# First layer's modulation by VectorE row sums instead of narrow matmuls, and its gate and branch weights' low parts by adding transfers

## The chip, the core and the metric

The kernel runs on one core of a Trainium2 chip. The metric is the device time of one execution in microseconds, as the median of several runs. A core has TensorE (PE, with a queue PEld that loads weights), VectorE (DVE), ScalarE (ACT), GpSimd (POOL) and SyncE (SP), which work in parallel, each in the order of its own queue, and sixteen DMA engines that move data between the main memory (HBM) and the on-chip SBUF. In this kernel plain transfers are issued by SP, and adding transfers, which add their source onto what lies at their destination, by POOL.

## The reference, cut to what matters

Two layers over 256 latent tokens `x` and 256 context tokens `xc`, 1024 channels wide. Per layer, all in float32:

```python
mod = s_lat @ w_ada[l] + b_ada[l]      # silu(c) @ (1024 x 6144); mod_c likewise from c_ctx
sh1, sc1, g1, sh2, sc2, g2 = split(mod, 6)
h = rmsnorm(x) * (1 + sc1) + sh1       # hc likewise from xc
p = h @ w_in[l]                        # 1024 -> 4608: conv branch | q, k, v | two gates
y_conv = conv_branch(p[..., :1024])    # GLU, 31-tap depthwise conv, LayerNorm, swish, @ w_conv_out
y_attn = attention(q, k, v, ...) @ w_na_out[l]
x = x + g1 * ((sigmoid(gc) * y_conv + sigmoid(ga) * y_attn) @ w_out[l])
h2 = rmsnorm(x) * (1 + sc2) + sh2
x = x + g2 * conv_ffn(h2)              # 1024 -> 5632, width-3 conv, gate, 2816 -> 1024
```

In the first layer the context tokens go the same way; in the last they serve only as keys and values. The output is the latent stream after a last RMSNorm.

The change concerns the modulation vectors `mod` of the first layer, from `g1` up to `sc2`, for both streams (two vectors of 1024 by a 1024 x 1024 block for each of the three parts), and the way in which the first layer's gate, attention-projection and convolution-projection weights are made ready for TensorE.

## The kernel before, in words

**Weights and products.** Activations lie with the channels on the 128 partitions. All weights but the modulation's come as units of 128 x 1024 float32 (512 KB): `U_IN + t` is tile `t` of the input projection (`T_GATE + n`, `t` = 14 to 29, are the sixteen gate tiles), `U_NA`, `U_CO` and `U_WO` are the attention, convolution and output projections. Each unit is loaded into a `raw` place (four of them) and split into a high part `whi` and a low part `wlo` (four places each), and each product is three matmuls (`mm3`, L187 to L189): high by high, high by low, low by high. For 512 tokens a gate unit is one `group` of 24 matmuls of 512 columns; a branch unit (`branch`) holds two groups of 12.

**Two ways to a low part.** `wunit` casts on ACT (L168) and subtracts on DVE (L169). `wadded` casts on ACT (L206), writes the negated high part into `wlo` on ACT (L207), and has POOL issue a transfer that adds `raw` onto it (L208). `unit8` chooses by the set `ADDED`. Before, it holds the first 19 tiles of the first layer's input projection (up to the fifth gate) and some of the second layer's. Branch units always take `wunit`.

**Two ways to the modulation.** `ada_all` computes a chunk of 256 outputs for both streams on TensorE: two units loaded into `raw`, sixteen matmuls of 32 output rows each (`ada_half`, L220), a copy on ACT (`ada_rows`, L239), two transposes and a small sum on DVE (`ada_sums`, L246 to L256). `ada_dots` computes a tile of 128 outputs on DVE: one unit is loaded (L155, in `raw_unit`), and for each stream one `tensor_tensor_reduce` (L289) multiplies it by the broadcast vector (`sb0`, made by `across`) and sums along the row straight into `mods`. In the first layer, chunks 0 to 7 (shift and scale of the first norm) are done at the start by TensorE and are not touched; chunks 8 to 12 (tiles 16 to 25) by `ada_all`, and tiles 26 to 39 by `ada_dots`.

**Order.** The program is written out in one stream, and its scheduler gives each engine its queue. Background work consists of generators in `side`; each `slot()` advances all of them by one step, and a group of 512 columns has two slots. `pace[0]` sets how many row sums `ada_dots` may do per slot: for two streams, a pace of 1.2 makes 0.6 tiles a slot. In the first layer the stretch around the change is: the last eleven gates (with the convolution's taps and LayerNorm as background work), the attention projection `U_NA` into the gates (L980), the convolution projection `U_CO` and the merge into `z` (L985 to L988), then the output projection `U_WO`, four units for both streams and four units for one stream after the other, with the residual (L993) that reads `g1`. `finish(g1)` runs what is left of the row sums before the second norm, which needs `sc2` and `sh2`.

Of the kernel before, what the change touches and what calls it, by code (L numbers as in the profile page):

```python
# [8 lines left out]
F32 = mybir.dt.float32  # L9
# [6 lines left out]
P = 128  # L16
# [3 lines left out]
S = 256  # L20
# [11 lines left out]
UW = 1024  # L32
# [11 lines left out]

U_GLU0, U_V, U_IN, U_NA, U_CO, U_WO, U_UP, U_DN = 0, 2, 6, 36, 40, 44, 52, 96
NU = 118
ADDED = {*((0, U_IN + i) for i in range(19)), *((1, U_IN + i) for i in (7, 8, 9, 14, 15, 16, 17))}
T_GLU, T_Q, T_K, T_GATE = 0, 6, 10, 14

SWAP16 = [(i + 16) % 32 for i in range(32)]  # L50
# [3 lines left out]
def trunk(ctx: ExitStack, tc: tile.TileContext, xt, cvec, crow, wall, wada, params, bias_t, rope_t, out):  # L54
# [34 lines left out]
    def add_side(gen):  # L89
        side.append(gen)  # L90
# [168 lines left out]
    def ada_all(chunks, rest=0):  # L259
        for l, j in chunks:  # L260
            ev = ada_rows(ada_products(l, j, "sc"))
            yield
            yield
            ada_sums(l, j, ev)
            for _ in range(rest):
                yield
# [9 lines left out]
    pace = [1.0]  # L276
# [336 lines left out]
    for l in range(DEPTH):  # L613
# [5 lines left out]
        with ExitStack() if last else start as e1a:  # L619
# [81 lines left out]
            with ExitStack() as e1b:  # L701
# [191 lines left out]
                n = 0  # L893
# [16 lines left out]
            with ExitStack() as e1c:  # L910
                ec = e1c.enter_context(tc.tile_pool(name=f"ec{l}", bufs=1))

                if l == 0:
                    sb0 = [across(ec, s) for s in range(2)]

                    def ada_more():
                        yield from ada_all([(0, 8)])
                        yield from ada_dots(0, range(26, 40), sb0)

                    pace[0] = 0.6  # L920
                    g1 = ada_more()
                    add_side(g1)
                sh_ = [ec.tile([P, T], F32R, name=f"sh{l}_{j}") for j in range(KC)]
                sl_ = [ec.tile([P, T], F32R, name=f"sl{l}_{j}") for j in range(KC)]

                def layer_norm():

                    while taps:
                        for _ in range(6 if last else 5):
                            if taps:  # L930
                                conv_tap(*taps.pop(0))
                        yield
                    pace[0] = 1.0 if last else 0.6
                    flat = [c.rearrange("p s t -> p (s t)") for c in cb]
                    sm = tp.tile([P, 512], F32, tag="ss", name=nm("ss"))
                    eng = pool if last else dve
                    eng.tensor_tensor(sm[:, :T], flat[0], flat[1], ALU.add)
                    eng.tensor_tensor(sm[:, :T], sm[:, :T], flat[2], ALU.add)
                    dve.tensor_tensor(sm[:, :T], sm[:, :T], flat[3], ALU.add)
                    yield  # L940
                    pm = psum("po")
                    pe.matmul(pm[:, :T], one.to_broadcast([P, P]), sm[:, :T], start=True, stop=True)
                    (s2,) = sum_squares(1, T)
                    for j in range(KC):
                        dve.scalar_tensor_tensor(flat[j], pm[:, :T], -1.0 / CONV, flat[j], ALU.mult, ALU.add)
                        s2.add(flat[j], j == KC - 1)
                    for _ in range(2 if last else 4):
                        yield
                    pb = yield from rstd(s2, CONV, "po")
                    for j in range(KC):  # L950
                        sg = tmp()
                        g, b = pr(l, LNG + j, 1), pr(l, LNB + j, 1)
                        dve.scalar_tensor_tensor(flat[j], flat[j], g, pb[:, :T], ALU.mult, ALU.mult)
                        act.activation(sg[:, :T], flat[j], AF.Sigmoid, bias=b)
                        dve.scalar_tensor_tensor(flat[j], flat[j], b, sg[:, :T], ALU.add, ALU.mult)
                        act.copy(sh_[j], flat[j])
                        dve.tensor_tensor(sl_[j], flat[j], sh_[j].bitcast(F32), ALU.subtract)
                        yield
                    pace[0] = 0.4 if last else 0.6

                side.remove(conv)
                ln = layer_norm()
                add_side(ln)
                for n in range(n, 2 * KD):
                    gate(ec, n, False)


                z = h_tiles()
                if not last:
                    g2 = ada_all([(0, j) for j in range(9, 13)], 4)  # L970
                    add_side(g2)

                def branch(base, xh, xl):
                    for n in range(0, KD, 2):
                        w = wunit(l, base + n // 2)
                        for i in range(2):
                            yield n + i, group(psum(), [cols(w, 4 * i + k) for k in range(KC)], xh, xl, ALL)

                for n, pa in branch(U_NA, oh, ol):
                    dve.tensor_tensor(gates[KD + n], pa[:, :T], gates[KD + n], ALU.mult)  # L980
                finish(ln)
                pace[0] = 0.0
                for n, pc in branch(U_CO, sh_, sl_):
                    t = tmp()[:, :T]
                    dve.tensor_tensor(t, pc[:, :T], gates[n], ALU.mult)  # L985
                    dve.tensor_tensor(t, t, gates[KD + n], ALU.add)
                    act.copy(z[0][n][:, :T], t)
                    dve.tensor_tensor(z[1][n][:, :T], t, z[0][n][:, :T].bitcast(F32), ALU.subtract)  # L988


                def residual(ss_, ps, part, n, s, off):
                    c = slice(s * S, (s + 1) * S)
                    dve.scalar_tensor_tensor(x[n][:, c], ps[:, off : off + S], mod(l, part, n, s), x[n][:, c], ALU.mult, ALU.add)  # L993
                    ss_.add(x[n][:, c], n == KD - 1)

                h2 = z

                RAW = slice(S, 2 * S + 2)

                def plain(k):  # L1000
                    hi, lo = z[0][k][:, CTX], z[1][k][:, CTX]
                    g = gains[l, 4][:, k, 0:1]
                    lastev[0] = act.activation(hi, x[k][:, LAT], AF.Identity, scale=g)
                    dve.scalar_tensor_tensor(lo, x[k][:, LAT], g, hi.bitcast(F32), ALU.mult, ALU.subtract)

                def plain_shift(k):
                    hi, lo = (z[i][k][:, 2 * S : 2 * S + 2] for i in range(2))
                    b = mod(l, 3, k, 0).to_broadcast([P, 2])
                    act.copy(hi, b)
                    dve.tensor_tensor(lo, b, hi.bitcast(F32), ALU.subtract)  # L1010

                if not last:
                    finish(g2)
                sss = sum_squares(NS, S)
                if last:
                    for k in range(KD):
                        gain(l, 4, N2G, k, 1)
                        plain_shift(k)
                NB = KD if last else KD // 2
                for n in range(NB):  # L1020
                    ps = group(psum(), unit8(l, U_WO + n), *z, ALL)
                    for s in range(NS):
                        residual(sss[s], ps, 2, n, s, s * S)
                    if last:
                        plain(n)
                    elif n == 0:
                        pace[0] = 0.8
                pace[0] = 0.3
                held = [unit8(l, U_WO + n) for n in range(NB, KD)]
                for s in range(NS if held else 0):  # L1030
                    for n, w in zip(range(NB, KD), held):
                        c = slice(s * S, (s + 1) * S)
                        ps = psum()
                        for k in range(KD):
                            mm3(ps[:, c], w[k], z[0][k][:, c], z[1][k][:, c], k == 0, k == KD - 1)
                            if k % 4 == 3:
                                slot()
                        residual(sss[s], ps, 2, n, s, s * S)
                    if s == 0:
                        finish(g1)  # L1040
                        nl = norm(l, sss[0], 4, 3, N2G, h2, (0,))
                        add_side(nl)
# [187 lines left out]
def _ada_units(w):  # L1230

    import numpy as np

    u = np.ascontiguousarray(w.transpose(0, 2, 1)).reshape(DEPTH, 48, P, UW).copy()
    u[0, :16] = w[0][:, : 2 * D].reshape(2, 4, P, 2, 8, P).transpose(4, 0, 2, 1, 3, 5).reshape(16, P, UW)
    u[0, 16:26] = w[0].reshape(2, 4, P, 24, S).transpose(3, 0, 2, 1, 4)[8:13].reshape(10, P, UW)
    return u


# [90 lines left out]
```

## Time and profile before

| | |
|---|---|
| median of 3 runs | 1120.04 us (1119.17 to 1121.54) |
| profiled execution, its own time | 1121.22 us |
| its span in the profile | 1119.4 us |
| granted TensorE clock, mean | 0.997 |
| HBM read | 187.63 MB, 169 GB/s over the span |
| loads by SP (plain) | 190.77 MB in the queue q1 |
| adding transfers by POOL | 26 of 512 KB, 13.63 MB in the queue q0 |

In a row by line, "x1328 | 446.7, 337" is count, busy time in us and mean ns of one; behind the next bar stands the idle time of the engine just before, and what ended it. In a row of order in time the first two numbers are start and duration. A row of a stage has its bounds, its length, and then the busy time of each engine with the number of instructions. A row of waits has the total, the number of times, and the longest. Durations of matmuls overlap: the time that one costs PE is the distance between starts. The DMA share is the mean busy share of the sixteen engines.

### The profile page before, as it was taken

What the parts mean: (1) busy time and instruction counts of PE and PEld (TensorE: products, weight loads), DVE (VectorE), ACT (ScalarE), POOL (GpSimd) and SP (SyncE); (2) the same over time, 40 slices, a digit from 0 to 9 for tenths busy, and PEclk for the clock granted to TensorE, in tenths of its full rate; (3) what the DMA queues carried; (4) which work ended last, traced back from release to release, by engine and by line L of the source; (5) the groups of instructions that cost most, each with busy time, mean ns of one, the idle gap of its engine ahead of it and who ended that gap; (6) DMA issues with size and microseconds to landing.
All of it is one profiled execution on the core that took longest, in us unless ns stands there. A gap on an engine that the chain in (4) does not pass through costs nothing.

```text
span 1119.4 us, 18214 instructions
## 1 busy us (share of the span) xinstructions
PE 1103.7 (99%) x6988; PEld 954.0 (85%) x6988; DVE 886.9 (79%) x1615; ACT 582.8 (52%) x968; POOL 36.2 (3%) x50
## 2 busy tenths in 40 slices
PE   9999999999999999999999999999999999999997
PEld 7777777787789988888888788998899999999997
DVE  5579899875878788887997655789699898988773
ACT  3458878541334543434334222545778667666642
POOL 1011110000000000000000000000100000000000
PEclk9999999999999999999999999999999999999998
DMA  9988662554743354544556666566864474666781
GB/s 345 298 191 228 146 166 82 188 166 158 256 136 116 114 166 143 176 157 144 169 173 205 207 192 206 183 201 193 230 180 148 154 254 161 192 196 179 219 271 57
DMA packets 59223, 205.60 MB, mean 184 GB/s; under 512 B 7168, under 2 KB 7424, under 8 KB 59136
## 3 DMA queue, kind: packets, MB, share of 16 engines
q1 hardware_dynamic: 55104, 190.77, 53.6%
q0 software_dynamic: 3744, 13.63, 6.3%
q8 instruction: 55, 0.90, 0.3%
q14 instruction: 32, 0.26, 0.1%
q10 hardware_dynamic: 288, 0.04, 0.0%
HBM read 187.63 MB, written 1.05 MB: 169 GB/s over the span
## 4 chain that ended last, share of the span: by engine, by line
PE 83%; DVE 7%; ACT 5%; DMA 3%; issue 1%; SPq 1%; DVEq 0%; ACTq 0%
PE main L187 24%; PE main L189 24%; PE main L188 24%; PE main L724 4%; DMA raw<-in_wall 2%; DVE cb L654 2%; SPq L716 1%; DVE wlo L169 1%; PE sc L187 1%; PE sc L189 1%; PE sc L188 1%; PE po L555 1%; ACT whi L168 1%; PE po L220 1%; DMA x<-in_xt 1%
## 5 line engine op out<-in xcount | busy, mean ns | idle before, releaser
L187 PE MATMUL main<-h,whi 128*128 128x256 f32 (+1 forms) x1328 | 446.7, 337 | 0.0
L189 PE MATMUL main<-h,wlo 128*128 128x256 f32 (+1 forms) x1328 | 442.9, 335 | 1.1 <-DVE wlo L169 1.1
L188 PE MATMUL main<-h,whi 128*128 128x256 f32 (+1 forms) x1328 | 442.4, 334 | 0.1
L168 ACT CAST whi<-raw 128x1024 fp32r<-128x1024 f32 (+1 forms) x218 | 225.4, 1038 | 261.2 <-DMA raw<-in_wall 139.6
L169 DVE TENSOR_TENSOR wlo<-raw,whi 128x1024 fp32r<-128x1024 f32 (+1 forms) x218 | 262.4, 1209 | 100.6 <-ACT whi L168 99.1
L187 PEld LDWEIGHTS main<-h,whi 128*128 128x128 f32 x1328 | 249.4, 188 | 30.7 <-issue 2.6
L189 PEld LDWEIGHTS main<-h,wlo 128*128 128x128 f32 x1328 | 249.3, 188 | 29.6 <-DVE wlo L169 1.5
L188 PEld LDWEIGHTS main<-h,whi 128*128 128x128 f32 x1328 | 249.8, 188 | 28.7 <-DVE h L385 0.5
L654 DVE SCALAR_TENSOR_TENSOR cb<-u,par,cb 128x512 f32<-128x512 f32 (+1 forms) x240 | 144.9, 618 | 3.0
L289 DVE CUSTOM_DVE_ANT_0 t<-raw,sb,par 128x1024 bf16<-128x1024 f32 x100 | 126.7, 1279 | 2.2 <-DMA raw<-in_wada 2.2
L189 PE MATMUL main<-fh,wlo 128*128 128x256 f32 (+1 forms) x386 | 123.0, 319 | 0.4 <-DVE wlo L169 0.4
L188 PE MATMUL main<-fl,whi 128*128 128x256 f32 (+1 forms) x386 | 123.0, 319 | 0.0
L187 PE MATMUL main<-fh,whi 128*128 128x256 f32 (+1 forms) x386 | 122.9, 319 | 0.0
L189 PEld LDWEIGHTS main<-fh,wlo 128*128 128x128 f32 x386 | 72.7, 188 | 6.4 <-DVE wlo L169 0.9
L187 PEld LDWEIGHTS main<-fh,whi 128*128 128x128 f32 x386 | 72.7, 188 | 5.6
L188 PEld LDWEIGHTS main<-fl,whi 128*128 128x128 f32 x386 | 72.7, 188 | 5.6
L1058 ACT ACTIVATE t<-main,par 128x512 f32<-128x512 f32 (+1 forms) x82 | 50.7, 668 | 28.0 <-PE main L189 28.0
L1059 DVE SCALAR_TENSOR_TENSOR t<-main,par,t 128x510 f32<-128x510 f32 (+1 forms) x82 | 47.5, 615 | 7.0 <-ACT t L1058 6.7
L1062 DVE SCALAR_TENSOR_TENSOR t<-main,par,t 128x510 f32<-128x510 f32 (+1 forms) x82 | 46.6, 610 | 0.0
L384 ACT ACTIVATE h<-t,mod 128x256 fp32r<-128x256 f32 x56 | 25.4, 502 | 37.6 <-DVE t L383 37.6
L724 PE MATMUL main<-whi,h 128*128 128x512 f32 x128 | 40.5, 402 | 0.1
L1084 ACT CAST fh<-t 128x256 fp32r<-128x256 f32 (+1 forms) x43 | 21.9, 510 | 34.6 <-DVE t L1074 34.2
(224 smaller groups left out, 1253.2 us busy)
## 6 DMA issues: line engine op xcount, KB each, us to landing
raw<-in_wall SPq DMA_DIRECT2D x239, 512.0 KB, 4.3
raw<-in_wada SPq DMA_DIRECT2D x88, 512.0 KB, 4.6
wlo<-raw POOLq DMA_DIRECT2D x26, 512.0 KB, 5.8
bias<-in_bias_t SPq DMA_DIRECT2D x8, 520.0 KB, 5.5
row<-in_wada SPq DMA_DIRECT2D x8, 512.0 KB, 5.3
sb<-in_crow SPq DMA_DIRECT2D x5, 512.0 KB, 5.7
x<-in_xt SPq DMA_DIRECT2D x8, 256.0 KB, 4.5
raw<-in_wall SPq DMA_DIRECT2D x8, 256.0 KB, 7.9
```

The lines of the kernel that those rows point to most:

```text
L168: act.copy(hi[:, c], r[:, c])
L169: dve.tensor_tensor(lo[:, c], r[:, c], hi[:, c].bitcast(F32), ALU.subtract)
L187: pe.matmul(ps, w[0], xh, start=start, stop=False)
L188: pe.matmul(ps, w[0], xl, start=False, stop=False)
L189: pe.matmul(ps, w[1], xh, start=False, stop=stop)
L289: dve.tensor_tensor_reduce(tmp().bitcast(BF16), r, v, 1.0, pr(l, BADA + n, 1), ALU.mult, ALU.add, mods[l][:, n, s : s + 1])
L384: high = act.activation(hi[:, c], y[:, c], AF.Identity, bias=b)
L654: dve.scalar_tensor_tensor(cb[j], src, w, cb[j], ALU.mult, ALU.add)
L724: mm = pe.matmul(pv[t], h1[n == 1][k][:, c], w[n == 2][:, b], start=k + n == 0, stop=k == KD - 1 and n == 2)
L1058: act.activation(c, pv_, AF.Identity, bias=pr(l, FDB + t, 1), scale=w[1])
L1059: dve.scalar_tensor_tensor(c[:, :, 1:], pv_[:, :, : S - 1], w[0], c[:, :, 1:], ALU.mult, ALU.add)
L1062: dve.scalar_tensor_tensor(c[:, :, : S - 1], pv_[:, :, 1:], w[2], c[:, :, : S - 1], ALU.mult, ALU.add)
```

## The change

Row sums on VectorE take over tiles 16 to 25 of the first layer's modulation: `ada_dots` runs from tile 16 to 39, with the paces changed to 1.2 in the gates, 0.7 in `U_NA` and 0.2 in `U_CO`. Its loads get two places of their own (`own`) instead of the four `raw` ones. The five chunks of `ada_all` with their matmuls, copies and transposes are gone there. The first layer's remaining eleven gate units and its eight `U_NA` and `U_CO` units get their low parts by adding transfers. The layout of the modulation's weights follows (tiles 16 to 25 lie as those after them).

```diff
-ADDED = {*((0, U_IN + i) for i in range(19)), *((1, U_IN + i) for i in (7, 8, 9, 14, 15, 16, 17))}
+ADDED = {*((0, U_IN + i) for i in range(30)), *((1, U_IN + i) for i in (7, 8, 9, 14, 15, 16, 17))}
...
                     sb0 = [across(ec, s) for s in range(2)]
 
-                    def ada_more():
-                        yield from ada_all([(0, 8)])
-                        yield from ada_dots(0, range(26, 40), sb0)
-
-                    pace[0] = 0.6
-                    g1 = ada_more()
+                    own = lambda: ec.tile([P, UW], F32, tag="own", bufs=2, name=nm("own"))
+                    pace[0] = 1.2
+                    g1 = ada_dots(0, range(16, 40), sb0, own)
                     add_side(g1)
...
-                    pace[0] = 1.0 if last else 0.6
+                    pace[0] = 1.0 if last else 1.2
...
-                    pace[0] = 0.4 if last else 0.6
+                    if last:
+                        pace[0] = 0.4
...
                 z = h_tiles()
-                if not last:
-                    g2 = ada_all([(0, j) for j in range(9, 13)], 4)
-                    add_side(g2)
 
                 def branch(base, xh, xl):
                     for n in range(0, KD, 2):
-                        w = wunit(l, base + n // 2)
+                        w = wunit(l, base + n // 2) if last else wadded(l, base + n // 2)
...
+                if not last:
+                    pace[0] = 0.7
                 for n, pa in branch(U_NA, oh, ol):
...
                 finish(ln)
-                pace[0] = 0.0
+                pace[0] = 0.0 if last else 0.2
                 for n, pc in branch(U_CO, sh_, sl_):
...
-                if not last:
-                    finish(g2)
                 sss = sum_squares(NS, S)
...
-    u[0, 16:26] = w[0].reshape(2, 4, P, 24, S).transpose(3, 0, 2, 1, 4)[8:13].reshape(10, P, UW)
```

## The prediction

> **What bounds the kernel now.** I read the page first (sums by engine, chain), then the engines by stage around the change, then the waits of that stretch, then TensorE in order of time, then DMA by stage. In the page:
>
> ```profile
> PE 1103.7 (99%) x6988; PEld 954.0 (85%) x6988; DVE 886.9 (79%) x1615; ACT 582.8 (52%) x968; POOL 36.2 (3%) x50
> ...
> PE 83%; DVE 7%; ACT 5%; DMA 3%; issue 1%; SPq 1%; DVEq 0%; ACTq 0%
> ```
>
> TensorE is busy for 99% of the span, and 83% of the chain that ended last is its work. The change touches the stretch from layer 0's sixth gate to the middle of its output projection, here cut at the gates, the attention projection (U_NA), the convolution projection (U_CO) and the start of the output projection (columns: PE, PEld, DVE, ACT, POOL, granted clock, DMA share, GB/s):
>
> ```profile
> 197.00:262.00 65.00, 65.00 (x297) 51.73 (x297) 46.22 (x68) 28.68 (x40) 1.96 (x1) 1.00 0.49 162
> 262.00:290.00 28.00, 27.24 (x155) 19.94 (x154) 19.05 (x36) 4.77 (x7) 0.00 (x0) 1.00 0.69 231
> 290.00:314.00 24.00, 24.00 (x118) 19.03 (x117) 20.83 (x32) 11.22 (x15) 0.00 (x0) 1.00 0.64 212
> 314.00:348.00 34.00, 34.00 (x201) 29.79 (x200) 25.78 (x50) 9.36 (x18) 0.00 (x0) 1.00 0.43 124
> ```
>
> PE is full, at a granted clock of 1.00; DVE, ACT and DMA have room. The waits between 196 and 348 us hold a single line in which PE's matmuls stood for somebody:
>
> ```profile
> ACT whi L168 <- PE main L188: 26.8, 12, 5.0
> ...
> PE main L189 <- DVE wlo L169: 0.8, 1, 0.8
> ```
>
> The first line says that the preparation of weights runs ahead: twelve times ACT stood at a whi place that PE had not yet given back, so units are made ready as early as four places allow. So here time is what PE executes, and a microsecond taken off PE is a microsecond of the kernel, as long as nothing new is late for PE.
>
> **What the change takes off PE.** Five chunks of the modulation (8 to 12 of layer 0) go: each is 16 narrow matmuls (L220) and, later, two transposes (L246) among the wide ones. One of them, in order of time on PE:
>
> ```profile
> 263.06 0.40 PE L189 MATMUL main<-oh,wlo 128*128 128x512 f32 x1
> 263.39 1.07 PE L220 MATMUL sc<-raw,sil 128*32 128x256 f32 x16
> 264.39 0.50 PE L187 MATMUL main<-oh,whi 128*128 128x512 f32 x1
> 264.73 0.39 PE L188 MATMUL main<-ol,whi 128*128 128x512 f32 x1
> ...
> 267.04 0.39 PE L189 MATMUL main<-oh,wlo 128*128 128x512 f32 x1
> 267.27 0.38 PE L246 MATMUL pt<-ident,t 128*128 128x128 f32 x2
> 267.40 0.48 PE L187 MATMUL main<-oh,whi 128*128 128x512 f32 x1
> 267.72 0.40 PE L188 MATMUL main<-ol,whi 128*128 128x512 f32 x1
> ```
>
> Durations overlap, so I go by starts. From 264.73 to 267.04 lie ten wide matmuls: 0.231 us each. From 263.06 to 264.73 are two such steps (0.46) in 1.67 us: the 16 narrow matmuls cost 1.21. From 267.04 to 267.72 are two steps in 0.68 us: the transposes cost 0.22. Together 1.43 us a chunk, 5 x 1.43 = 7.1 us.
>
> The one wait is also in this stretch:
>
> ```profile
> 276.50 0.39 PE L188 MATMUL main<-ol,whi 128*128 128x512 f32 x1
> 277.65 0.50 PE L189 MATMUL main<-oh,wlo 128*128 128x512 f32 x1 [0.76 <-DVE wlo L169]
> ```
>
> 1.15 us between two starts instead of 0.23: 0.9 us. A low part of a branch unit came late, from VectorE. After the change no low part before U_WO is VectorE's, and the modulation's loads no longer take two of the four raw places at a time until PE has read them. It goes, unless an added transfer is late in its stead. The most that can be won is 7.1 + 0.9 = 8.0 us.
>
> **What the change adds, and what hides it.** Prices, from the groups by form:
>
> ```profile
> L169 DVE TENSOR_TENSOR wlo<-raw,whi 128x1024 fp32r<-128x1024 f32 x212 | 258.4, 1224 | 100.3 <-ACT whi L168 99.1 <-PE po L942 0.2
> L289 DVE CUSTOM_DVE_ANT_0 t<-raw,sb,par 128x1024 bf16<-128x1024 f32 x100 | 126.7, 1279 | 2.2 <-DMA raw<-in_wada 2.2
> L207 ACT ACTIVATE wlo<-whi 128x1024 fp32r<-128x1024 f32 x26 | 27.7, 1065 | 0.4
> L289 DVE DVE_READ_ACCUMULATOR2_ANT mod<- 128x1 f32 x108 | 8.9, 83 | 0.0
> L208 POOL DMA_DIRECT2D wlo<-raw x26 | 22.8, 877 | 197.8 <-ACT wlo L207 94.1 <-PE pt L246 34.0 <-ACT qk L864 31.9
> ```
>
> VectorE: row sums for tiles 16 to 39 instead of 26 to 39, ten tiles for two streams: 20 x (1.279 + 0.083) = 27.2 us more. Eleven gate units and eight branch units lose their subtraction: 19 x 1.224 = 23.3 us less. Net +3.9 us, with five reductions, five bias adds and no more evictions on ACT to set against it. By stage:
>
> ```profile
> 197.00:262.00 65.00, 12.77 (x11) 1.00 0.49 162
> ...
> 197.00:262.00 65.00, 15.05 (x24) 1.00 0.49 162
> 262.00:290.00 28.00, 10.13 (x16) 1.00 0.69 231
> ```
>
> The first line is L169, the others L289; 24 rows are twelve sums with their read-outs, six tiles, so a tile is 2.51 us. A pace of 1.2 gives 0.6 tiles a slot; the eleven gates have 22 slots, 12 tiles or 30.1 us. VectorE then has 46.2 - 12.8 - 15.1 + 30.1 = 48.4 us in a stage of 11 x 24 x 0.231 = 61 us. In U_NA (16 slots at 0.7, 5.6 tiles) it has 14.1 us of sums and what it had beside its 10.1 us of sums and its subtractions, some 5 us, in 22 us. Both fit, though U_NA only just. What VectorE gives PE there is a free bank (L980), and three further banks cover 3 x 12 x 0.231 = 8.3 us of lateness. I take zero.
>
> ACT: 19 x 1.065 = 20.2 us more, over some 105 us in which it is at most half busy. POOL: 19 issues of 0.88 us on an idle engine. I take zero for both.
>
> SP: ten tiles' loads (512 KB each) replace the same ten units of the chunks, but wait for one of two places of their own. The wait that this takes away and the one that stays, among SP's waits between 200 and 300 us:
>
> ```profile
> SPq L155 <- PE sc L220: 13.4, 4, 8.3
> ...
> SPq L155 <- DVE mod L289: 4.4, 3, 2.2
> ```
>
> Behind a modulation load in SP's queue stand the weight loads. Before, they stood up to 8.3 us behind a load that waited for the narrow matmuls. Afterwards they stand behind one that waits for the row sum two tiles earlier; the waits for a sum here are 2.2 us at the longest. Between 0 and the ten loads times 2.2 us, less the 13.4 that go; a raw place is filled some four units (22 us) ahead, so I take zero.
>
> DMA is the term that is not zero. A few microseconds in layer 1 where plain loads and adding transfers run together (775 to 800 us), and the gates stage as it is:
>
> ```profile
> q1 hardware_dynamic: 995, 3.65, 46.8%
> q0 software_dynamic: 576, 2.10, 43.5%
> raw<-in_wall SPq DMA_DIRECT2D x7, 512.0 KB, 5.8
> wlo<-raw POOLq DMA_DIRECT2D x5, 512.0 KB, 7.3
> ...
> q1 hardware_dynamic: 2880, 10.49, 48.9%
> raw<-in_wada SPq DMA_DIRECT2D x9, 512.0 KB, 4.5
> raw<-in_wall SPq DMA_DIRECT2D x9, 512.0 KB, 4.0
> ```
>
> An adding transfer costs 0.435 x 25 us / 2.10 MB x 0.524 MB = 2.7 us of all sixteen engines; a load costs 0.489 x 65 / 10.49 x 0.524 = 1.6 us. Gates and U_NA together: 15 units x (1.6 + 2.7) + 17.6 tiles x 1.6 = 93 us in 84 us of PE. That is 9 us too much, a tenth. Against it stand the cushions. A whi place comes free four units ahead, 3 x 5.5 = 16.6 us before PE needs it; cast, negated copy, issue and a landing of 7.3 us take 1.05 + 1.07 + 0.88 + 7.3 = 10.3 us; 6.3 us are left. The raw place ahead of it has about as much again, and modulation tiles may lag without PE noticing. In the 25 us quoted, 5.8 and 7.3 us to landing with the engines 90% taken made no wait of PE. I take 1.5 us of PE waiting for an added low part, nearer to nothing than to the 9 us; the ends are 0 and 9.
>
> The Trainium skill, "DMA: Bandwidth & Descriptors", section "Anatomy of one DMA", gives a fixed 2 us and bytes over 436 GB/s. At that rate 512 KB occupy the engines for 1.2 us, an estimate, loads and adds alike, and the same sum is 15 x 2.4 + 17.6 x 1.2 = 57 us of 84: no excess, and the full 8.0 us. The trace does not agree for adding transfers, 2.7 us each.
>
> **The sum.** 8.0 - 1.5 = 6.5 us. The profiled execution took 1121.22 us for a span of 1119.4; it becomes 1114.7. It lies 1.2 us above the median of the runs, 1120.04, and so the median becomes 1113.5 us. PE stays full after 348 us, so nothing later takes it back. About 0.2%, 2.2 us, is what a measurement here can tell from no change.
>
> **Rivals.** *Everything is hidden*: the DMA excess is taken up by the cushions, 8.0 us, 1112.0. For it: PE waits for no added low part in the trace of before. It is the good end of my case. *VectorE becomes the bound in U_NA*: it works in order, and a sum whose tile has not landed holds the L980 behind it. If VectorE enters U_NA more than the 8.3 us of three banks late, PE waits. Its 48.4 us of 61 speak against this. It would return 3 to 5 us: 1117. *The sixteen DMA engines become the bound*, which ends on the other side: in gates and U_NA every unit takes what its transfers take. It decides once the backlog is over the 6.3 us of the whi places and the lag of the tiles doesn't help, since their loads stand ahead of the weights' in SP's queue. Priced by the rows: 9 us of excess and, because a late unit also holds its raw place and the next load behind it, about 3 us more in refilling: 12 - 8.0 = 4 us slower, 1124. For it: 69% of the engines' time was already taken in U_NA before any adding transfer. Against: those in layer 1 at 90% without a wait. The same page, section "Issuing engines are not separate DMA queues", says that transfers issued by different engines interleave on the same sixteen, which would make POOL's transfers lengthen SP's; the trace agrees as far as it goes, with loads landing in 5.8 us beside adds and 4.0 without.
>
> **How the numbers follow.** My case with its good end, 1111.5 to 1116: 0.60. VectorE, 1116 to 1119: 0.15. DMA as the bound, 1119 to 1128: 0.25, of which 0.05 under 1122.3. Faster by over 0.2% (under 1117.8): 0.60 and most of the second, 0.70. Slower (over 1122.3): 0.20. Between: 0.10. The range of 8 in 10 leaves a little below 1111 and the upper end of the DMA case: 1111 to 1123. The forecast's own range is 1111.5 to 1116.
>
> **What would show it.** In the profile after: no L220 on bank sc after 60 us and 16 transposes of L246 instead of 26; 45 added transfers instead of 26; L169 with 19 fewer; 128 row sums in all, over both forms. Right: PE has under 2 us of idle time between 197 and 340 us, all for wlo by DMA. Wrong by DMA: the share in gates and U_NA is near 1.0, landings of wlo over 10 us, and PE waits for them. Wrong by VectorE: PE waits for L980. Wrong in the first term: U_NA starts less than 1.2 us earlier after the gates, which hold one chunk.

## The result, and the profile after

The changed kernel takes 1132.05 us (median of 6 runs, 1130.02 to 1134.8) against 1121.32 us before (6 runs, 1119.17 to 1123.27). The ratio is 1.0097, interval 1.008 to 1.0114: slower by 10.7 us, where 1113.5 us was forecast. The profiled execution has a span of 1130.4 us, 11.0 more than before.

The sums and the chain, from the page of the changed kernel:

```profile
PE 1100.1 (97%) x6898; PEld 954.0 (84%) x6898; DVE 889.0 (79%) x1626; ACT 599.1 (53%) x982; POOL 52.8 (5%) x69
...
PE 76%; issue 7%; DVE 5%; DMA 5%; ACT 5%; SPq 1%; POOL 0%; POOLq 0%; DVEq 0%; ACTq 0%
```

TensorE is busy for 3.6 us less, and for 97% of the span instead of 99%: it stands. By stage (length, PE, PEld, DVE, ACT, POOL, granted clock, DMA share, GB/s):

```profile
197.00:219.00 22.00, 22.00 (x95) 17.43 (x94) 15.01 (x25) 16.93 (x23) 3.89 (x5) 1.00 0.98 252
219.00:234.00 15.00, 8.26 (x40) 6.69 (x39) 7.82 (x14) 4.98 (x6) 3.56 (x3) 0.83 0.87 264
234.00:268.00 34.00, 34.00 (x145) 27.40 (x144) 19.85 (x32) 17.48 (x24) 4.57 (x6) 0.98 0.94 235
268.00:278.00 10.00, 10.00 (x46) 8.18 (x44) 5.00 (x8) 4.48 (x5) 1.76 (x2) 1.00 1.01 282
278.00:289.00 11.00, 1.70 (x7) 1.09 (x6) 8.44 (x14) 2.10 (x2) 0.86 (x1) 0.75 1.01 295
289.00:302.00 13.00, 13.00 (x49) 10.44 (x48) 10.81 (x20) 2.21 (x3) 0.86 (x1) 0.82 0.76 236
```

There are two holes in PE, one in the gates and one in U_NA, with the DMA engines at 0.87 to 1.01, and VectorE far from full: 5.0 us of 10 just ahead of the second hole. The waits between 196 and 360 us name both holes, and what VectorE stood for:

```profile
DVE t L289 <- DMA own<-in_wada: 36.0, 13, 6.0
...
PE main L187 <- DVE g L977: 9.3, 1, 9.3
...
PE po L369 <- POOL rs L364: 6.7, 1, 6.7
```

I read the first line as the cause and the two others as its effect; the experiments below test this. VectorE waited 36 us in thirteen times for modulation tiles that had not landed in `own`. In the order of its queue (L977 is the merge of attention into the gates, L980 before the change; L362 is the LayerNorm's step that POOL's L364 waits for):

```profile
227.78 1.28 DVE L289 CUSTOM_DVE_ANT_0 t<-own,sb,par 128x1024 bf16<-128x1024 f32 x1 [4.30 <-DMA own<-in_wada]
...
230.20 0.15 DVE L362 TENSOR_SCALAR red<-pt 128x4 f32<-128x4 f32 x1
...
278.20 1.29 DVE L289 CUSTOM_DVE_ANT_0 t<-own,sb,par 128x1024 bf16<-128x1024 f32 x1 [3.67 <-DMA own<-in_wada]
...
285.23 1.28 DVE L289 CUSTOM_DVE_ANT_0 t<-own,sb,par 128x1024 bf16<-128x1024 f32 x1 [2.11 <-DMA own<-in_wada]
...
287.64 0.68 DVE L977 TENSOR_TENSOR g<-main,g 128x512 f32<-128x512 f32 x1
```

And on PE:

```profile
225.37 0.40 PE L189 MATMUL main<-h,wlo 128*128 128x512 f32 x1
232.50 1.11 PE L369 MATMUL po<-ident,rs 128*128 128x128 f32 x4 [6.74 <-POOL rs L364]
233.27 0.78 PE L187 MATMUL main<-h,whi 128*128 128x512 f32 x1
...
278.69 0.40 PE L189 MATMUL main<-oh,wlo 128*128 128x512 f32 x1
288.38 0.80 PE L187 MATMUL main<-oh,whi 128*128 128x512 f32 x1 [9.30 <-DVE g L977]
288.98 0.63 PE L188 MATMUL main<-ol,whi 128*128 128x512 f32 x1
289.40 0.63 PE L189 MATMUL main<-oh,wlo 128*128 128x512 f32 x1
```

A short L362 stands behind sums whose tile lands late; POOL's root and PE's transposes stand behind L362. In U_NA the first L977, which would free the first of four banks, runs at 287.64. PE fills all four banks and stands for 9.3 us. No matmul waited for an added low part.

PE then runs on at half clock. The stages after the first hole, after the second, and once it is over (the granted clock is the third number from the right):

```profile
233.27:235.84 2.57, 2.57 (x9) 2.04 (x7) 2.18 (x4) 1.38 (x2) 0.97 (x2) 0.54 0.70 104
...
288.38:293.70 5.32, 5.32 (x13) 4.16 (x14) 4.84 (x7) 0.00 (x0) 0.00 (x0) 0.50 0.91 270
293.70:300.00 6.30, 6.30 (x29) 5.18 (x28) 4.53 (x10) 2.12 (x2) 0.86 (x1) 1.00 0.62 226
```

The account: 6.7 us and 9.3 us of standing; 5.3 us at a clock of 0.50 is 2.7 us lost, and the 2.6 us from 233.27 on at 0.54 another 1.2. That is 19.9 us, less the 8.0 us that the chunks and the old wait had cost: 11.9 us, against 11.0 in the spans; the 0.9 us between them is not accounted for.

### The profile page after: what moved, and what is told of

It is laid out like the page before. It is cut to its first block, busy times and chain, and to the rows that moved or that the text cites. A ratio compares the mean times of both kernels' runs of the same rounds, so it can differ in the third digit from the quotient of the medians.

```text
span 1130.4 us, 18121 instructions
## 1 busy us (share of the span) xinstructions
PE 1100.1 (97%) x6898; PEld 954.0 (84%) x6898; DVE 889.0 (79%) x1626; ACT 599.1 (53%) x982; POOL 52.8 (5%) x69
## 4 chain that ended last, share of the span: by engine, by line
PE 76%; issue 7%; DVE 5%; DMA 5%; ACT 5%; SPq 1%; POOL 0%; POOLq 0%; DVEq 0%; ACTq 0%
PE main L187 22%; PE main L188 22%; PE main L189 22%; PE main L724 4%; DMA own<-in_wada 3%; DVE cb L654 2%; DMA raw<-in_wall 1%; SPq L716 1%; DVE t L289 1%; PE sc L189 1%; PE sc L188 1%; PE po L555 1%; PE sc L187 1%; ACT whi L206 1%; ACT wlo L207 1%
## 5 line engine op out<-in xcount | busy, mean ns | idle before, releaser
L168 ACT CAST whi<-raw 128x1024 fp32r<-128x1024 f32 (+1 forms) x199 | 205.6, 1037 | 221.8 <-DMA raw<-in_wall 107.7
L169 DVE TENSOR_TENSOR wlo<-raw,whi 128x1024 fp32r<-128x1024 f32 (+1 forms) x199 | 238.8, 1207 | 88.5 <-ACT whi L168 87.3
L289 DVE CUSTOM_DVE_ANT_0 t<-raw,sb,par 128x1024 bf16<-128x1024 f32 x72 | 91.5, 1278 | 0.3 <-DMA raw<-in_wada 0.3
L289 DVE CUSTOM_DVE_ANT_0 t<-own,sb,par 128x1024 bf16<-128x1024 f32 x48 | 60.2, 1280 | 36.0 <-DMA own<-in_wada 36.0
L206 ACT CAST whi<-raw 128x1024 fp32r<-128x1024 f32 x45 | 47.2, 1050 | 64.5 <-PE main L188 44.2
L1054 DVE SCALAR_TENSOR_TENSOR t<-main,par,t 128x510 f32<-128x510 f32 (+1 forms) x82 | 47.5, 615 | 11.1 <-ACT t L1053 10.6
L208 POOL DMA_DIRECT2D wlo<-raw x45 | 39.3, 881 | 306.2 <-ACT wlo L207 187.3
L207 ACT ACTIVATE wlo<-whi 128x1024 fp32r<-128x1024 f32 x45 | 47.8, 1062 | 0.6
```

Of the source, the lines that this page charges most:

```text
L168: act.copy(hi[:, c], r[:, c])
L169: dve.tensor_tensor(lo[:, c], r[:, c], hi[:, c].bitcast(F32), ALU.subtract)
L206: act.copy(hi, r)
L207: act.mul(lo, hi.bitcast(F32), -1.0)
L289: dve.tensor_tensor_reduce(tmp().bitcast(BF16), r, v, 1.0, pr(l, BADA + n, 1), ALU.mult, ALU.add, mods[l][:, n, s : s + 1])
L1054: dve.scalar_tensor_tensor(c[:, :, 1:], pv_[:, :, : S - 1], w[0], c[:, :, 1:], ALU.mult, ALU.add)
```

## The experiments

Theories. **A**: the adding transfers fill the sixteen DMA engines, tiles land late, and VectorE, working in order, holds PE's next step behind a sum whose tile is missing. **B**: VectorE has too many sums, whatever DMA does. **C**, after the first four: time is lost in SP's queue, where a modulation load stands behind a weight load whose raw place an adding transfer holds.

**e1: the row sums without the adding transfers.**

```diff
-ADDED = {*((0, U_IN + i) for i in range(30)), ...
+ADDED = {*((0, U_IN + i) for i in range(19)), ...
-                        w = wunit(l, base + n // 2) if last else wadded(l, base + n // 2)
+                        w = wunit(l, base + n // 2)
```

> The change without its adding transfers: the eleven gate units and the eight branch units get their low parts by VectorE's subtraction again; the row sums from tile 16 on and their two own places stay. Theory A (the sixteen DMA engines are full, modulation tiles land late, and VectorE, which works in order, holds PE's next step behind a sum whose tile is missing): DMA share between 200 and 290 us falls from 0.94 to about 0.65, VectorE's waits for own fall from 36 us to under 8, the two PE waits (for L977 and for L369) go, and the five chunks' 7.1 us are won: 1114 us. Theory B (VectorE simply has too many sums in the gates and U_NA, whatever DMA does): VectorE has 23 us more work than in the changed kernel, PE waits for L977 as long or longer: 1130 us or more.

1112.53 us, ratio to before 0.9917 (0.9902 to 0.9931): faster by 8.8 us. Among its waits (190 to 345 us), and two of its stages:

```profile
DVE t L289 <- DMA own<-in_wada: 2.6, 5, 0.9
```

```profile
200.00:250.00 50.00, 50.00 (x221) 40.27 (x220) 48.58 (x74) 25.59 (x34) 1.04 (x1) 1.00 0.65 204
250.00:300.00 50.00, 50.00 (x220) 40.89 (x219) 47.01 (x72) 13.47 (x17) 0.00 (x0) 1.00 0.69 211
```

VectorE is busy for 96 of 100 us, more than in any other kernel here, and the waits list none of PE between 190 and 360 us. B falls: a VectorE that is full does no harm, one that waits does.

**e2: the adding transfers without the row sums**: the kernel before with the two changed lines above the other way round.

> The kernel before with the nineteen adding transfers alone: chunks 8 to 12 stay on TensorE, row sums from tile 26 at the old paces. Theory A: the bytes are the same as in the changed kernel, so the engines are again over 0.9 busy and something of the modulation or a low part is late: PE waits 3 to 10 us, 1124 to 1131 us. Theory B: VectorE is relieved by 23 us and nothing else is in the way: 1120 to 1121 us, the old 0.9 us wait gone.

1143.62 us, 1.0192 (1.0177 to 1.0207), the slowest of all. Its waits of PE (190 to 360 us), and of SP's queue (195 to 320 us):

```profile
PE main L189 <- DMA wlo<-raw: 9.0, 5, 3.8
PE sc L220 <- DMA raw<-in_wada: 2.5, 2, 1.6
```

```profile
SPq L155 <- DMA wlo<-raw: 76.0, 14, 10.2
```

Here the low parts themselves are late. The four raw places serve weights and modulation, and an adding transfer holds one until it has landed, so SP stood 76 us. Slower, as A said, but by more than its 3 to 10 us, and at a DMA share of 0.86 from 200 to 250 us and 0.76 from 250 to 300: the engines were not full, where A expected over 0.9. That made C worth a test.

**e3: sums and adding transfers, but few loads.**

```diff
-            r = raw_unit(wada[l, n], place())
+            if kept is not None and len(kept) == 2:
+                r = kept[n % 2]
+            else:
+                r = raw_unit(wada[l, n], place())
+                if kept is not None:
+                    kept.append(r)
```

> The changed kernel with all its row sums and adding transfers, but only the first two modulation tiles of the stretch are loaded and the other 22 sums read these again (left out: 22 loads of 512 KB, so mods from tile 18 on are of the wrong tiles). Theory A: without 22 x 1.6 = 35 us of DMA work the engines are 0.6 busy, no wait for own, no PE wait: 1113 us. Theory B: VectorE's work is the same as in the changed kernel: 1130 us.

1113.9 us, 0.9925 (0.991 to 0.994). Two of its stages:

```profile
200.00:250.00 50.00, 50.00 (x221) 40.14 (x220) 43.14 (x73) 32.77 (x45) 9.88 (x10) 1.00 0.95 221
250.00:300.00 50.00, 50.00 (x219) 40.90 (x218) 35.07 (x59) 20.90 (x24) 6.09 (x7) 1.00 0.78 183
```

Same sums, same adding transfers, no wait of PE: with its tiles in place VectorE hurts nobody. B falls again. A had the time, but not the share: it expected 0.6, and without the tiles the engines were still busy for 0.95 and 0.78.

**e4: an even pace.**

```diff
-                    pace[0] = 1.2
+                    pace[0] = 0.8
-                    pace[0] = 1.0 if last else 1.2
+                    pace[0] = 1.0 if last else 0.8
-                    pace[0] = 0.7
+                    pace[0] = 0.8
-                pace[0] = 0.0 if last else 0.2
+                pace[0] = 0.0 if last else 0.8
```

> The changed kernel with the row sums spread evenly: pace 0.8 in the gates, U_NA and U_CO instead of 1.2, 0.7 and 0.2. Theory A: gates and U_NA ask for 15 x 4.3 + 15.2 x 1.6 = 89 us of DMA in 84 instead of 93, and the rest moves to U_CO, where adding transfers end; part of the waits goes: 1118 to 1126 us. Theory B: fewer sums in the gates but more in U_NA (6.4 tiles instead of 5.6) and U_CO (6.4 instead of 1.6, beside 16 us of merging in 22): the wait for L977 stays and one in U_CO comes, 1130 us or more.

1136.22 us, 1.0127 (1.0108 to 1.0146). Waits of PE:

```profile
PE main L187 <- DVE g L977: 9.9, 1, 9.9
PE main L187 <- DVE t L982: 8.2, 3, 3.0
```

The wait in the gates is gone, the one in U_NA is as long, and U_CO's merge (L982) has three of its own. A expected an improvement and was wrong here; I read it as tiles moved to where PE's banks depend on VectorE. B's two waits and its 1130 us or more came true. But VectorE waited 32.3 us for `own` in this run as well, so late tiles explain it too, and it does not bring back B, which e1 and e3 rule out.

**e5: half of each tile.** As in e3, with the branch that reuses a place loading its first half:

```diff
+                r = kept[n % 2]
+                lastdma[0] = sp.dma_start(r[:, : UW // 2], wada[l, n][:, : UW // 2])
```

> The changed kernel, but from the third modulation tile of the stretch on only half of each tile is loaded (256 KB instead of 512; left out: the other halves, so those sums mix tiles). Loads, their order in SP's queue, the adding transfers and the sums are as many as in the changed kernel. Theory A (the sixteen engines' time is what runs out): 22 x 0.8 = 18 us less to carry, 75 us in 84, VectorE's waits for own fall under 6 us, no PE wait: 1113 to 1116 us. Theory C (time runs out in SP's queue: a modulation load stands behind a weight load that waits for a raw place which an adding transfer still holds): the order is unchanged, own still comes late, VectorE waits over 20 us, 1125 us or more.

1124.98 us, 1.0037 (1.0022 to 1.0052). **e6: four places of their own.** One line, `bufs=2` to `bufs=4` in `own`:

> The changed kernel with four own places instead of two, so that a modulation load may be issued two tiles further ahead. Theory A: the bytes are the same and the engines stay over 0.9 busy; the lead is used up within the gates; VectorE still waits over 15 us for own: 1123 to 1131 us. Theory C: with two tiles (some 9 us) of lead the waits behind weight loads are covered: under 8 us of waits for own, 1113 to 1118 us.

1122.01 us, 1.0004 (0.9991 to 1.0016). What VectorE and PE waited for in e5, and then in e6 (L983, L375 and L370 there and L977, L369 and L364 here are the same statements):

```profile
DVE t L295 <- DMA own<-in_wada: 22.9, 9, 4.3
...
PE po L375 <- POOL rs L370: 4.5, 1, 4.5
...
PE main L187 <- DVE g L983: 2.0, 2, 1.7
```

```profile
DVE t L289 <- DMA own<-in_wada: 17.2, 7, 5.6
...
PE main L187 <- DVE g L977: 4.5, 1, 4.5
```

They give back a third and a half of the loss: 7 us and 10 us of the 19.5 between 1132.05 and 1112.53. Half tiles land in 4.0 us in the median between 197 and 290 us instead of 6.6, and still VectorE waits 22.9 us, as C said and A did not. With four places, and so more tiles under way at once, a tile takes 10.5 us to land, and still VectorE waits less. A had e6's wait (over 15 us) and C did not (under 8); the time fell between their two ranges.

**e7 and e8: adding transfers for the gates only, and for the branches only** (e7 has the second of e1's two edits, e8 the first).

> The changed kernel with adding transfers for the eleven gate units only; U_NA and U_CO get their low parts by VectorE again. Theory A: the gates ask for 11 x 4.3 + 12 x 1.6 = 66 us in 61, U_NA for 15 in 22: tiles are late in the gates and the LayerNorm step L362 behind them, so PE's wait for L369 stays in part, the one for L977 goes: 1116 to 1123 us. Theory C: the same places are held in the gates, with the same result; this run shows the size of the gates' part.

> The changed kernel with adding transfers for the eight branch units only; the eleven gates get their low parts by VectorE again. Theory A: the gates ask for 37 us in 61, U_NA for 4 x 4.3 + 5.6 x 1.6 = 26 in 22, and the cushions take that: 1112 to 1116 us. Theory C: in U_NA weight loads stand behind adding transfers and modulation loads behind these; PE waits 3 to 9 us for L977: 1117 to 1123 us.

1125.64 us, 1.0034 (1.0018 to 1.0049), and 1123.51 us, 1.0028 (1.0014 to 1.0042). PE's waits of e7 and then of e8:

```profile
PE po L369 <- POOL rs L364: 7.0, 1, 7.0
```

```profile
PE main L187 <- DVE g L977: 5.9, 3, 4.6
```

Each half of the adding transfers makes the hole of its own stage, and either is enough to turn 8.8 us of gain into a loss. In e7 the wait for L369 stayed whole, not in part, and the time is above A's 1116 to 1123 us. In e8 A's 1112 to 1116 us was wrong: the cushions did not take it. C's wait of 3 to 9 us for L977 came true, with a time 0.5 us above its range.

**f1 and f2: loads by another queue, and a fifth raw place**: the 24 loads by `act.dma_start` instead of `sp.dma_start`; then `bufs=5` for `raw`.

> The changed kernel with the 24 modulation loads issued by ACT's queue instead of SP's: bytes, places and sums as they were, but no modulation load stands behind a weight load any more. Theory C (place in SP's queue): VectorE waits under 12 us for own and PE under 5 us: 1113 to 1119 us. Theory A (the engines' time): own is as late as before, VectorE waits over 25 us: 1127 to 1134 us. In between: both have a share. ACT may itself be held by a load that waits for its place.

> The changed kernel with five raw places instead of four (in the whole kernel, so other stages may shift by a microsecond or two). Theory C: a weight load waits less for a raw place that an adding transfer holds, and the modulation loads behind it come sooner: VectorE waits under 20 us for own, 1117 to 1126 us. Theory A: no fewer bytes, 1128 to 1133 us.

1126.07 us, 1.0038 (1.0021 to 1.0055), and 1131.35 us, 1.0077 (1.0049 to 1.0106). What VectorE waited for in the one and in the other:

```profile
DVE t L293 <- DMA own<-in_wada: 33.1, 11, 4.7
```

```profile
DVE t L289 <- DMA own<-in_wada: 32.2, 9, 5.3
```

SP's queue alone is not it: with no weight load ahead of them the tiles landed after 9.1 us in the median (197 to 230 us), just as late as the 9.0 of the changed kernel, and the fifth place changed little, as A had said. f1's time lies between the two ranges. ACT, holding loads that waited for their place, was late itself with casts (18.3 us behind sums, in four times), and PE waited 3.2 us for added low parts, so f1's time is no clean measure of C.

**f3: row sums through the raw places**, e1 without `own`:

> Row sums from tile 16 on, no adding transfers beyond those of before, and no own places: the tiles go through the four raw places. It tells what the own places do in e1_sums_only (1112.5 us). If they matter, weight loads wait for raw places that hold modulation tiles, and PE waits for a low part as before the change: 1114 to 1118 us. If not: 1112 to 1113 us.

1119.47 us, 0.9989 (0.9968 to 1.0009): no difference from before, and neither of the two ranges. The places of their own are worth 7 us in e1; without them PE waits 2.8 us for L364, is at a granted clock of 0.50 from 223 to 229 us, and waits in smaller pieces; 0.4 us of these is for a low part, so the wait that was forecast is not what costs.

**f4: four places and half tiles together.**

> e5_half_tiles and e6_four_places in one: four own places, and from the fifth tile of the stretch on only half of each tile is loaded (left out: the other halves). If engine time and lead each have a share of the loss and nothing else has: VectorE waits under 6 us for own, PE under 1 us, 1112 to 1115 us. If something else holds PE: 1118 us or more.

1112.76 us, 0.9918 (0.9887 to 0.995). VectorE's wait for tiles, and the stage of U_NA:

```profile
DVE t L295 <- DMA own<-in_wada: 8.5, 5, 3.8
```

```profile
260.00:280.00 20.00, 20.00 (x89) 16.37 (x88) 15.12 (x28) 8.01 (x9) 2.98 (x4) 1.00 1.04 288
```

With the DMA engines as full as ever (1.04) and every adding transfer in place, PE stands for 0.2 us, and the whole gain is there, though VectorE waits 8.5 us and not under 6. So full engines alone are not the loss either. It is the turn-round of a tile: a load may be issued only when the sums two tiles earlier are done, may then stand in its queue, and then takes long to land beside adding transfers. In the median that was 9.0 us for the loads issued from 197 to 230 us and 8.1 us from 230 to 262, where e1 has 4.2. With 2.5 us of sums, two places make at these medians a tile every 5.8 and 5.3 us; in e1 it is 3.4. Fifteen tiles stand in VectorE's queue ahead of the first L977. They took from 206.80 to 287.64, 5.4 us each, where 4.3 would have brought L977 at 270.6, as early as PE could use it; e1's fourteen took 4.1 each. The lag comes from the gates: when PE began U_NA, ten of the fifteen were done, where in e1 twelve of the fourteen were done and the next was under way. In U_NA the loads landed in 5.1 us (262 to 290 us) and the last four tiles followed each other every 4.0 us (269.22 to 285.23), which is what U_NA asks for (22 us for 5.6).

How much of the turn-round is the queue's can be read in the changed kernel. Of the thirteen loads issued from 211 to 281 us ten went out within 0.1 us of the end of the sums that freed their place. Three, all in the gates, stood behind weight loads for 2.0, 2.6 and 5.0 us. The 5.0 us are those of the tile that VectorE waited for at 227.78, ahead of L362:

```profile
215.23 0.08 DVE L289 DVE_READ_ACCUMULATOR2_ANT mod<- 128x1 f32 x1
215.99 4.18 SPq L155 DMA_DIRECT2D raw<-in_wall  x2
220.28 3.56 SPq L155 DMA_DIRECT2D own<-in_wada  x2
```

Its place was free at 215.31, its load went out at 220.28 and took 7.5 us to land. So the queue has 9.6 us in all, the landings have the rest. What each costs PE by itself stays open: e5 shortened the one, f1 the other, and neither was enough.

## Why the prediction was wrong, point by point

- **What bounds the kernel, and the 8.0 us**: right. With the row sums alone (e1) 8.8 us are gained.
- **The late low part** (1.5 us taken, 0 to 9 the ends): wrong place. In the changed kernel PE waited for no added low part; the cushions of the whi and raw places held. In e2, where the modulation loads take raw places too, they did not (9.0 us).
- **"Modulation tiles may lag without PE noticing"**: this is the step that failed. A lagging tile stops VectorE, and behind it in the same queue stood L362 and L977. The wait of 2.2 us at the longest for a sum, from which SP's term was taken at zero, belonged to a kernel whose loads landed in 4.5 us.
- **VectorE, taken at zero**: it was judged by its busy time, 48.4 us of 61, when its idle time counted. (The sum was a little low besides: 22 slots at 0.6 are 13.2 tiles, not 12, and it set the work of a stage of 65 us against 61.) The three banks' 8.3 us of lateness was the right measure: the four U_NA groups that fill the banks end on PE at 278.9 us, so the first ends 8.3 us earlier, at 270.6, and L977 came 17 us later; 17 - 8.3 is 9 us, the 9.3 us of the wait. The rival had mechanism and threshold right; its 0.15 was too small, and its 3 to 5 us left out the gates and the half clock.
- **The DMA sum**, 93 us in 84: right in size; the shares by stage were 0.87 to 1.01 where it said over 1. At the 436 GB/s of the Trainium skill's "DMA: Bandwidth & Descriptors", section "Anatomy of one DMA", there would by the estimate have been no excess and the full 8.0 us: the measured shares speak against it, as the 2.7 us did. (That fit is the page's for transfers issued by GpSimd; most of those here are SP's loads.) The rival of full engines came nearest in time (1124, up to 1128), and by chance: its path was late units, and what was late in the changed kernel were tiles.
- **"What would show it"**: the counts hold (45 added transfers, 128 sums, 199 subtractions), and so does the sign for VectorE, PE waiting for L977. Of the sign for DMA only the share came, not the low parts over 10 us (8.7 in the median) nor PE waiting for them. The sign for a wrong first term misleads: U_NA starts 6 us later than before (267.92 against 261.91), but through the hole in the gates; in e1 it starts 1.6 us earlier.
- **The clock** was not in the sum: 3.9 us of the 19.9.

## What to carry to other kernels

When a load is moved to an engine that works in order, ask what stands behind it in that engine's queue, and whether places divided by (time in the queue + landing + use) keep up with the pace; the landing to put in is that under the new load on DMA, not the old one. A busy share says nothing of this: e1 does well with VectorE 96% busy, the changed kernel badly with 61% from 197 to 289 us. Of two edits made together, try each alone: here one wins 8.8 us with its own places (1112.53 us, the best version found), the other loses 22.

## What the runs showed of the hardware

A pause of TensorE costs more than itself. After 6.7 and 9.3 us without matmuls the granted clock was 0.54 and 0.50 for 2.6 and 5.3 us, with matmuls 0.43 us apart instead of 0.23. In f3 2.8 us without matmuls (221.05 to 223.84) were enough: the clock was 0.50 from 223 to 229 us. After the 0.9 us wait in the kernel before nothing of the kind is seen (1.00 from 262 to 290 us). The Trainium skill, "TensorE: Matmul & The Clock Gate", section "What's actually happening", gives half clock after an idle window of some 3.4 us and full clock after as long a busy one. The two clocks agree, and so does the first pause's end, with full clock within 3.3 us of PE going on (232.50 to 235.84); the 5.3 us after the second pause are longer, and the 2.8 us of f3 are shorter than 3.4.

An adding transfer of 512 KB beside full loads took 8.7 us to land in the median in the changed kernel (5.4 to 12.5, from 196 to 330 us), and plain loads beside it were slower too: 9.0 us for a modulation tile from 197 to 230 us, against 4.3 in e1.
